# State-space parameters rebuilt: masks in ScalarE's copies, powers multiplied together, taps of four pairs on column groups, chunk matrices laid out by DMAs

## The chip, the cores and the metric

The kernel runs on one core of a Trainium2 chip. The metric is device time in microseconds (us) for one execution of the whole program, lower is better. TensorE multiplies matrices out of SBUF into PSUM; VectorE, ScalarE and GpSimd work on tiles; SyncE here only issues DMAs. In the profile these are PE (with PEld for its weight loads), DVE, ACT, POOL and SP. Each engine takes its instructions in program order and waits on semaphores for the others.

## The reference

Two networks run one after the other on 256 tokens of 1024 features. The first has two layers of differential attention and long convolutions. The second has four stages: an attention mixer, a dense feed-forward layer, an S5 state-space mixer and a mixture of eight experts. The change touches what prepares the S5 mixer. Cut to that:

```
def s5_mixer(h, w_in, lam_re, lam_im, log_dt, b_re, b_im, c_re, c_im, d_skip, w_glu, w_o):
    u = h @ w_in
    ug = u.reshape(B, S, 64 groups, 16)          # 64 states per group
    dt = exp(log_dt); mag = exp(lam_re * dt)
    a_re, a_im = mag * cos(lam_im * dt), mag * sin(lam_im * dt)
    f = (a - 1) / lam                            # complex
    bb = f[..., None] * b                        # complex, per group 64 x 16
    x[t] = a * x[t - 1] + bb @ ug[t]             # complex, by associative scan
    y = real part of (c @ x) + d_skip * u
    y = gelu(y); y = y * sigmoid(y @ w_glu)
    return y @ w_o
```

The kernel does not scan over 256 tokens. It takes four tokens as one step (64 steps), so it needs, for each pair of groups (128 states, 32 channels), matrices made of powers of `a`: input matrices `a^(3-s) * bb` for the tokens s = 0..3 of a step, output matrices `c * a^(t+1)`, and inside a step the taps `c * a^j * bb` for j = 0..3, with `d_skip` added at j = 0.

## The kernel before

All products with weights are done three times (high by high, high by low, low by high part), so each 128x1024 piece of a weight goes through one queue of work: a DMA on SP into `raw`, a copy on ACT into `whi` (L208), a subtraction on DVE into `wlo` (L211), then TensorE.

The dense feed-forward stage (`dense_ffn`) runs over eleven chunks of 256 hidden columns. For each it multiplies for gate and up (`proj_T`, L323 to L325, matmuls of 256 columns) and down (`mm3`, L221 to L223, 512 columns). Its four output accumulators hold four of the five PSUM buffers named `B`, so one is left for everything else. At the end of `proj_T` and of each down chunk a tick gives other generators a turn.

`s5_params` is such a generator. It is started with the stage at 0.7 steps to a tick and builds, for each quarter q of the 32 group pairs (8 pairs), four tables that are stored to DRAM and read back in the S5 stage behind it: sB (input matrices), sC (output matrices), sK (taps laid out as a 128x128 block triangular matrix per pair) and sT (rotations). One quarter before the change:

- `W`: the products of the powers with `bb`, by four calls of `cmul` (six DVE instructions each) on 128x128 elements; `W2` is a copy of `W` on ACT (L1467) for both groups of a pair.
- sB: 16 transposes of `W2` on TensorE (L1472), four to a PSUM buffer, taken out by DVE with a multiplication by a mask (L1474).
- sC: four more `cmul`, and 16 masked copies on ACT (L1488).
- sK: 16 matmuls of `W2` (128 weight columns) with the masked `c` (`s5cmk`, 32 columns) on TensorE (L1500), masked by DVE into `kj`; the skip term added there; a memset of `K` on POOL (L1515), and 10 copies of 32 partitions on ACT and DVE (L1520) that place the taps in the block triangle. One DMA from SP's queue stores it.
- sT: six levels of `cmul`, doubling the length, and a copy on ACT (L1531).

The modulation work of the first network (`adaln`, L959) is of interest too: there, too, a product of 32 weight columns by 128 moving columns is spread over four column groups of the array. Its small results go out by four DMAs from POOL's queue at a time (L965).

The tile framework orders instructions by a simulated time line, so code that is changed in one generator can also move its neighbours. The instructions of each engine keep the order it has chosen.

Of the kernel before, what the change touches and what calls it, by code (L numbers as in the profile page):

```python
# [15 lines left out]
ALU = mybir.AluOpType  # L16
# [102 lines left out]
class Net:  # L119
# [1261 lines left out]
    def s5_steps(self, sp, tp):  # L1381
# [59 lines left out]
        self.s5k = fr, fi, pw, sa, ca, mg4  # L1441

    def s5_params(self, sp):
# [4 lines left out]
        fr, fi, pw, sa, ca, mg4 = self.s5k  # L1448
        bm = self.load(sp, a["s5mask"], [P, 2, P], "s5mask", eng=self.dq)
        eye = self.load(sp, a["eye32"], [32, 32], "eye32", eng=self.dq)  # L1450
        dsk = self.load(sp, a["s5d"], [32, G], "s5d", eng=self.dq)
        for q in range(4):
# [5 lines left out]
            W = self.t(sp, [P, 2, 8, 4, 16], "s5W", bufs=2)  # L1458
# [9 lines left out]
            B = self.t(sp, [P, 8, 2, P], "s5st", bufs=2)  # L1468
# [10 lines left out]
            C = self.t(sp, [P, 8, 2, 4, 2, 16], "s5st", bufs=2)  # L1479
            m2 = bm[:, 1, :].rearrange("p (t g k) -> p t g k", t=4, g=2)[:, 0]  # L1480
            for t in range(4):
                p = pw[:, t + 1]
                cr, ci = self.t(sp, [P, 8, 16], "s5cr"), self.t(sp, [P, 8, 16], "s5ci")
                self.cmul(sp, [P, 8, 16], bc(p[:, 0, :], 16), bc(p[:, 1, :], 16), craw[:, 0], craw[:, 1], cr, ci, "s5cm",
                          neg_i=True)
                for ri, v in enumerate((cr, ci)):
                    for g in range(2):
                        nc.scalar.activation(C[:, :, ri, t, g, :], v, AF.Copy, scale=m2[:, g, 0:1])  # L1488
            self.dq.dma_start(self.sC[q], C.rearrange("p a b c d e -> p (a b c d e)"))
            yield  # L1490

            cm = self.t(sp, [P, 2, 8, 2, 16], "s5cmk")
            for g in range(2):
                nc.scalar.activation(cm[:, 0, :, g, :], craw[:, 0], AF.Copy, scale=m2[:, g, 0:1])
                V.scalar_tensor_tensor(cm[:, 1, :, g, :], craw[:, 1], -1.0,
                                       m2[:, None, g, :].broadcast_to([P, 8, 16]), ALU.mult, ALU.mult)
# [5 lines left out]
            kj = self.t(sp, [P, 8, 2, 16], "s5kj")  # L1502
            m3 = bm[:, 0, :].rearrange("p (g k) -> p g k", g=2)[:, :, :16]
            for g in range(2):
                V.tensor_tensor(kj[:, :, g, :], pt[:, :S].rearrange("p (i g k) -> p i g k", i=8, g=2)[:, :, g, :],
                                m3[:, None, g, :].broadcast_to([P, 8, 16]), ALU.mult)
            kj = kj.rearrange("p i g k -> p i (g k)")
            dd = self.t(sp, [P, 8, 32], "s5dd")[96:128]
            ey, dq = self.t(sp, [P, 32], "s5ey")[96:128], self.t(sp, [P, 8], "s5dq")[96:128]
            V.tensor_copy(ey, eye)  # L1510
            V.tensor_copy(dq, dsk[:, qs])
            V.tensor_tensor(dd, ey[:, None, :].broadcast_to([32, 8, 32]), dq[:, :, None].broadcast_to([32, 8, 32]), ALU.mult)
            V.tensor_tensor(kj[96:128], kj[96:128], dd, ALU.add)
            K = self.t(sp, [P, 8, P], "s5K")
            nc.gpsimd.memset(K, 0.0)  # L1515
# [556 lines left out]
```

## Time and profile before

| | |
|---|---|
| time, median of 3 runs | 1911.8 us (1909.59 to 1914.67) |
| the profiled execution | 1902.7 us, of which its span is 1900.2 us |
| TensorE (PE) busy | 1818.4 us, 96% of the span |
| VectorE (DVE) busy | 1554.9 us, 82% |
| ScalarE (ACT) busy | 1213.4 us, 64% |
| GpSimd (POOL) busy | 164.6 us, 9% |
| dense feed-forward stage | about 736 to 947 us of the span |
| S5 stage | about 947 to 1080 us, the experts behind it to the end |

Times in the views are counted from the span's start. The busy time of a matmul in the profile is its latency, and matmuls overlap; what one costs in a stream is the distance from its start to the next one's start, which the time line shows. "PEclk" is the clock that TensorE was granted as a share of 2.4 GHz.

### The profile page before, as it was taken

The page shows a single profiled execution, that of the slowest core. Times are in us where ns is not written, and L with a number is a line of the kernel's source. Part 1 is how long each engine was busy: PE and PEld are TensorE (multiplying, and loading weights), DVE is VectorE, ACT ScalarE, POOL GpSimd, SP SyncE. Part 2 cuts the span into 40 slices and gives each one's busy share as a digit, 9 for nine tenths or more (in the row PEclk, how much of TensorE's full clock was granted, in tenths as well). Part 3 has the DMA queues.
Part 4 walks back from the last instruction along what each step waited for, and adds up shares of the span by engine and source line. Part 5 has one row for each costly group of instructions (what it writes and reads, how often), then busy time and mean ns, then how long its engine had stood idle before and what let it go on. Part 6 is the DMA issues. An engine that isn't in the chain of part 4 may idle for free.

```text
span 1900.2 us, 31269 instructions
## 1 busy us (share of the span) xinstructions
PE 1818.4 (96%) x11358; PEld 1551.7 (82%) x11358; DVE 1554.9 (82%) x2646; ACT 1213.4 (64%) x1708; POOL 164.6 (9%) x297
## 2 busy tenths in 40 slices
PE   7999998999989998999989899999999999999996
PEld 6887776988878778999889788888888888888784
DVE  6887667687558669998678789999999999998996
ACT  5664355564448535555554677887778787877774
POOL 0003232231330000000000100000001000100000
PEclk9999998999999969999988999999999999999998
DMA  7656785876775504787675779999999999999990
GB/s 247 205 153 209 245 286 197 277 259 196 255 242 159 165 22 156 227 270 241 208 284 196 279 266 376 340 355 344 378 342 349 353 377 354 346 369 361 339 352 24
DMA packets 258539, 503.58 MB, mean 265 GB/s; under 512 B 23346, under 2 KB 101108, under 8 KB 256328
## 3 DMA queue, kind: packets, MB, share of 16 engines
q1 hardware_dynamic: 239384, 448.05, 68.7%
q0 software_dynamic: 18992, 53.45, 7.9%
q8 instruction: 91, 1.49, 0.3%
q14 instruction: 72, 0.59, 0.1%
HBM read 485.47 MB, written 15.75 MB: 264 GB/s over the span
## 4 chain that ended last, share of the span: by engine, by line
PE 78%; issue 10%; DVE 6%; DMA 4%; ACT 2%; POOL 0%; POOLq 0%; ACTq 0%; DVEq 0%
PE A L222 12%; PE A L221 12%; PE A L223 12%; PE B L221 6%; PE B L222 6%; PE B L223 6%; PE A L323 4%; PE A L325 4%; PE A L324 4%; PE B L959 2%; DMA rawm<-in_e_mod_mix_w_dram 2%; DVE wlo L211 1%; PE B L1754 1%; PE B L1101 1%; PE B L440 1%
## 5 line engine op out<-in xcount | busy, mean ns | idle before, releaser
L211 DVE TENSOR_TENSOR wlo<-raw,whi 128x1024 fp32r<-128x1024 f32 x777 | 930.8, 1222 | 183.7 <-ACT whi L208 172.0
L208 ACT ACTIVATE whi<-raw 128x1024 fp32r<-128x1024 f32 x777 | 814.3, 1058 | 344.6 <-PE A L223 137.7
L221 PE MATMUL A<-whi,hTh 128*128 128x512 f32 (+1 forms) x752 | 286.7, 389 | 7.5 <-ACT hTh L208 4.9
L222 PE MATMUL A<-wlo,hTh 128*128 128x512 f32 (+1 forms) x752 | 290.0, 386 | 1.3 <-DVE wlo L211 1.0
L223 PE MATMUL A<-whi,hTl 128*128 128x512 f32 (+1 forms) x752 | 287.5, 384 | 0.9 <-DVE hTl L211 0.9
L323 PE MATMUL A<-hTh,whi 128*128 128x256 f32 x864 | 246.2, 285 | 3.5 <-ACT hTh L208 2.6
L325 PE MATMUL A<-hTh,wlo 128*128 128x256 f32 x864 | 245.2, 284 | 0.0
L324 PE MATMUL A<-hTl,whi 128*128 128x256 f32 x864 | 244.1, 283 | 1.0 <-DVE hTl L211 1.0
L221 PEld LDWEIGHTS A<-whi,hTh 128*128 128x128 f32 x752 | 142.9, 190 | 38.8 <-ACT hTh L208 6.1
L323 PEld LDWEIGHTS A<-hTh,whi 128*128 128x128 f32 x864 | 165.4, 192 | 6.9 <-ACT hTh L208 2.8
L222 PEld LDWEIGHTS A<-wlo,hTh 128*128 128x128 f32 x752 | 143.1, 190 | 33.9 <-DVE wlo L211 4.8
L223 PEld LDWEIGHTS A<-whi,hTl 128*128 128x128 f32 x752 | 142.6, 190 | 31.2 <-DVE hTl L211 2.1
L324 PEld LDWEIGHTS A<-hTl,whi 128*128 128x128 f32 x864 | 165.3, 191 | 3.2 <-DVE hTl L211 1.2
L325 PEld LDWEIGHTS A<-hTh,wlo 128*128 128x128 f32 x864 | 165.1, 191 | 1.7 <-issue 1.2
L222 PE MATMUL A<-wlo,xg 128*128 128x512 f32 (+1 forms) x384 | 143.1, 373 | 0.3 <-DVE wlo L211 0.3
L223 PE MATMUL A<-whi,xg 128*128 128x512 f32 (+1 forms) x384 | 142.7, 372 | 0.0
L221 PE MATMUL A<-whi,xg 128*128 128x512 f32 (+1 forms) x384 | 141.2, 375 | 0.0
L222 PE MATMUL B<-wlo,mhh 128*128 128x512 f32 x352 | 138.6, 394 | 0.0
L223 PE MATMUL B<-whi,mhl 128*128 128x512 f32 x352 | 137.5, 391 | 0.0
L221 PE MATMUL B<-whi,mhh 128*128 128x512 f32 x352 | 120.6, 393 | 0.2 <-ACT mhh L208 0.2
L222 PEld LDWEIGHTS A<-wlo,xg 128*128 128x128 f32 x384 | 72.3, 188 | 13.4 <-DVE wlo L211 0.8
L223 PEld LDWEIGHTS A<-whi,xg 128*128 128x128 f32 x384 | 72.3, 188 | 12.5
(588 smaller groups left out, 2868.9 us busy)
## 6 DMA issues: line engine op xcount, KB each, us to landing
raw<-in_o_exp_up_dram SPq DMA_DIRECT2D x176, 512.0 KB, 5.7
raw<-in_o_exp_down_dram SPq DMA_DIRECT2D x176, 512.0 KB, 6.0
raw<-in_o_exp_gate_dram SPq DMA_DIRECT2D x174, 512.0 KB, 5.8
raw<-in_w_in_dram SPq DMA_DIRECT2D x96, 512.0 KB, 4.8
rawm<-in_e_mod_mix_w_dram POOLq DMA_DIRECT2D x24, 512.0 KB, 6.0
rawm<-in_e_mod_ffn_w_dram POOLq DMA_DIRECT2D x24, 512.0 KB, 5.7
rawm<-in_o_mod_mix_w_dram POOLq DMA_DIRECT2D x24, 512.0 KB, 5.6
rawm<-in_o_mod_ffn_w_dram POOLq DMA_DIRECT2D x24, 512.0 KB, 6.3
```

The costliest lines, as they stand in the source:

```text
L208: nc.scalar.activation(hi, src, AF.Copy)
L211: (nc.gpsimd if lo_eng == "pool" else nc.vector).tensor_tensor(lo, src, hi.bitcast(F32), ALU.subtract)
L221: nc.tensor.matmul(out, ah, bh, start=first, stop=False)
L222: nc.tensor.matmul(out, ah, bl, start=False, stop=False)
L223: nc.tensor.matmul(out, al, bh, start=False, stop=last)
L323: nc.tensor.matmul(o, wh[:, ms], xh[:, k, :], start=k == 0 and m == 0, stop=False, **kw)
L324: nc.tensor.matmul(o, wh[:, ms], xl[:, k, :], start=False, stop=False, **kw)
L325: nc.tensor.matmul(o, wl[:, ms], xh[:, k, :], start=False, stop=k == 7, **kw)
L440: nc.tensor.matmul(o, x[:, ks], dg, start=True, stop=True)
L959: nc.tensor.matmul(acc[32 * j:32 * j + 32, cs], silu[:, k:k + 1].broadcast_to([P, 32]), raws[i][:, k * P:(k + 1) * P], start=r == 0 and i ...
L1101: nc.tensor.matmul(pt[:, i, :], z[ps, ts], w[ps, ts], start=True, stop=True)
L1754: nc.tensor.transpose(ptr[:, i * P:(i + 1) * P], sg[:, i * P:(i + 1) * P], self.ident)
```

## The change

`s5_params` is rewritten, with one more table (`pr`, the powers in falling order) made at the end of `s5_steps`, and with new layouts of three small inputs (mask, unit matrix, skip weights).

- The masks for the two groups of a pair move into ACT's copies of `W` and `C` as a scale per partition (the helper `copy`). DVE's masked eviction of the transposes becomes a plain copy on ACT.
- The three powers of `W`, and the four of `C`, are multiplied in one `cmul` each, on 384 and 512 elements.
- The taps take 32 columns of `W2` as weights and 128 columns of `C` (now with a fifth slot for power 0) as moving data, and four pairs write to the four groups of 32 PSUM partitions.
- The block triangle is no longer built in SBUF. `K` holds three zero blocks and four taps per pair, and 16 DMAs on POOL's queue write shifted windows of it to sK.
- sT is built for two quarters at a time (`TQ = 2`), sC is stored by two DMAs.

```diff
+        pr = self.t(sp, [P, 2, G, 3], "s5pr")
+        for s in range(3):
+            V.tensor_copy(pr[:, :, :, s], pw[:, 3 - s])
...
+        copy = lambda o, i, m: nc.scalar.activation(o, i, AF.Copy, scale=gm[:, m:m + 1])
...
+            shape = [P, 8, 3, 16]
+            p = [pr[:, ri, qs, :, None].broadcast_to(shape) for ri in range(2)]
+            w = [W[:, ri, :, 3:4, :].broadcast_to(shape) for ri in range(2)]
+            self.cmul(sp, shape, *p, *w, W[:, 0, :, 0:3, :], W[:, 1, :, 0:3, :], "s5cw")
             yield
-            for s in range(3):
-                p = pw[:, 3 - s]
-                self.cmul(sp, [P, 8, 16], bc(p[:, 0, :], 16), bc(p[:, 1, :], 16), W[:, 0, :, 3, :], W[:, 1, :, 3, :],
-                          W[:, 0, :, s, :], W[:, 1, :, s, :], "s5cm")
...
             for g in range(2):
-                nc.scalar.copy(W2[:, :, :, :, g, :], W)
+                copy(W2[:, :, :, :, g, :], W, g)
...
-                V.tensor_tensor(B[:, i:i + 2].rearrange("p a b c -> p (a b) c"), pt.rearrange("p (n c) -> p n c", n=4),
-                                bm[:, None, 0, :].broadcast_to([P, 4, P]), ALU.mult)
+                nc.scalar.copy(B[:, i:i + 2].rearrange("p a b c -> p (a b) c"), pt.rearrange("p (n c) -> p n c", n=4))
...
+            self.cmul(sp, shape, *p, *c, cr, ci, "s5cw", neg_i=True)
+            for ri, v in enumerate((cr, ci)):
+                for g in range(2):
+                    copy(C[:, :, ri, 0, g, :], craw[:, ri], 2 * ri + g)
+                    copy(C[:, :, ri, 1:5, g, :], v, g)
+            for ri in range(2):
+                self.dq.dma_start(self.sC[q].rearrange("p (i r m) -> p i r m", i=8, r=2)[:, :, ri],
+                                  C[:, :, ri, 1:5].rearrange("p i t g k -> p i (t g k)"))
...
-            for i in range(8):
-                for ri in range(2):
-                    nc.tensor.matmul(pt[:, i * 32:(i + 1) * 32], W2[:, ri, i].rearrange("p s g k -> p (s g k)"),
-                                     cm[:, ri, i].rearrange("p g k -> p (g k)"), start=ri == 0, stop=ri == 1)
+            for h in range(2):
+                for ri in range(2):
+                    for i in range(4):
+                        nc.tensor.matmul(pt[32 * i:32 * i + 32, h * P:(h + 1) * P], W2[:, ri, 4 * h + i, 3].rearrange("p g k -> p (g k)"),
+                                         C[:, 4 * h + i, ri, 0:4].rearrange("p t g k -> p (t g k)"), start=ri == 0, stop=ri == 1,
+                                         skip_group_check=True)
+            K = self.t(sp, [P, 2, 7, 32], "s5K")
+            nc.gpsimd.memset(K[:, :, 0:3], 0.0)
+            nc.scalar.copy(K[:, :, 3:7], pt[:, :S].rearrange("p (h t m) -> p h t m", h=2, t=4))
+            for h in range(2):
+                V.scalar_tensor_tensor(K[:, h, 3], eye, dsk[:, 2 * q + h:2 * q + h + 1], K[:, h, 3], ALU.mult, ALU.add)
             for s in range(4):
-                for t in range(s, 4):
-                    j = 3 - (t - s)
-                    dst, src = K[s * 32:(s + 1) * 32, :, t * 32:(t + 1) * 32], kj[j * 32:(j + 1) * 32]
-                    (nc.scalar.copy if (s + t) % 2 else V.tensor_copy)(dst, src)
-            self.dq.dma_start(self.sK[q], K.rearrange("p a b -> p (a b)"))
+                for i in range(4):
+                    self.mq.dma_start(self.sK[q][s * 32:(s + 1) * 32].rearrange("k (h i m) -> k i h m", h=2, i=4)[:, i],
+                                      K[i * 32:(i + 1) * 32, :, 3 - s:7 - s].rearrange("k h t m -> k h (t m)"))
```

The order moves in three places of the feed-forward stage. First TensorE, third quarter: before, the taps (`s5cmk` by `s5W2`) stand between a down chunk (`B`, `fhh`) and a gate chunk (`A`, `hTh`).

```order
L221 MATMUL B_1607_8030<-whi_2000_9936,fhh_1987_9863 128x512
L222 MATMUL B_1607_8030<-wlo_2001_9937,fhh_1987_9863 128x512
L223 MATMUL B_1607_8030<-whi_2000_9936,fhl_1988_9864 128x512
L1500 MATMUL B_2003_9969<-s5cmk_2002_9964,s5W2_1948_9704 128x32 x16
L323 MATMUL A_2015_10021<-hTh_1575_7905,whi_2010_10011 128x256
L324 MATMUL A_2015_10021<-hTl_1576_7906,whi_2010_10011 128x256
```

The same place in the changed kernel:

```order
L221 MATMUL B_1608_8034<-whi_1888_9672,fhh_1875_9599 128x512
L222 MATMUL B_1608_8034<-wlo_1889_9673,fhh_1875_9599 128x512
L223 MATMUL B_1608_8034<-whi_1888_9672,fhl_1876_9600 128x512
L1505 MATMUL B_1890_9700<-s5C_1867_9573,s5W2_1854_9483 32x128 x16
L323 MATMUL A_1898_9750<-hTh_1576_7909,whi_1893_9740 128x256
L324 MATMUL A_1898_9750<-hTl_1577_7910,whi_1893_9740 128x256
```

The count (16) and the neighbours are the same; the shape turns from 128x32 to 32x128, and the masked `c` is now the first four slots of `C`.

Next ScalarE, third quarter, before: the weight copies (`whi`) stand among the masked copies that build sC in `s5st`.

```order
L208 ACTIVATE whi_1993_9875<-raw_1992_9873 128x1024
L1488 ACTIVATE s5st_1961_9794<-s5cr_1962_9795,s5mask_1641_8290 128x8x16 x2
L1488 ACTIVATE s5st_1961_9794<-s5ci_1963_9796,s5mask_1641_8290 128x8x16 x2
L1488 ACTIVATE s5st_1961_9794<-s5cr_1968_9811,s5mask_1641_8290 128x8x16 x2
L208 ACTIVATE whi_1997_9930<-raw_1996_9928 128x1024
```

In the changed kernel the copies that stand there, one to a weight copy, empty the PSUM buffers `B` of the transposes:

```order
L1481 COPY s5st_1855_9486<-B_1856_9487 128x512
L208 ACTIVATE whi_1881_9611<-raw_1880_9609 128x1024
L1481 COPY s5st_1855_9486<-B_1857_9493 128x512
L208 ACTIVATE whi_1885_9666<-raw_1884_9664 128x1024
L1481 COPY s5st_1855_9486<-B_1858_9499 128x512
L208 ACTIVATE whi_1888_9672<-raw_1887_9670 128x1024
```

ACT now releases the one free PSUM buffer, which DVE did before. On TensorE the groups of four transposes that take that buffer have 24 to 34 other matmuls between them within a quarter in the changed kernel (the first group of the second quarter is drawn out over more).

Last GpSimd at the end of the stage, before: after the last memset of `K` it goes on with the gate row of the S5 stage (`mgt`) and the first columns of its states (`s5X`).

```order
L1515 MEMSET s5K_2008_9996 128x1024
L1515 MEMSET s5K_2143_10638 128x1024
L201 DMA mgt_2224_10973<-rowo_mod_mix_776_3924 128x1024
L1585 MEMSET s5X0_2257_11179 128x8
L1585 MEMSET s5X1_2258_11180 128x8
```

The same place in the changed kernel:

```order
L1515 DMA sK_1313_6708<-s5K_1891_9717 64x1x128 x16
L1509 MEMSET s5K_2005_10358 128x2x96
L1515 DMA sK_1313_6708<-s5K_2005_10358 64x1x128 x16
L201 DMA mgt_2051_10567<-rowo_mod_mix_776_3924 128x1024
L1587 MEMSET s5X0_2084_10773 128x8
L1587 MEMSET s5X1_2085_10774 128x8
```

Sixteen DMAs per quarter now stand ahead of these on POOL's queue; the last taps on TensorE stand 48 rows, all of them down matmuls of 512 columns, ahead of the end of the stage (before, 95 rows).

## Rows read from the trace of the kernel before

**Rows 1.** The page's first part: busy us, share of the span, number of instructions.

```profile
PE 1818.4 (96%) x11358; PEld 1551.7 (82%) x11358; DVE 1554.9 (82%) x2646; ACT 1213.4 (64%) x1708; POOL 164.6 (9%) x297
```

**Rows 2.** Window: busy us of PE, PEld, DVE, ACT, POOL; clock; DMA; GB/s.

```profile
740.00:940.00 200.00, 200.00 (x1464) 189.38 (x1463) 172.84 (x490) 114.06 (x183) 3.65 (x12) 0.98 0.72 234
```

**Rows 3.** Groups by line in that stage: | busy us, mean ns | idle.

```profile
L323 PE MATMUL A<-hTh,whi 128*128 128x256 f32 x320 | 91.7, 287 | 0.0
...
L211 DVE TENSOR_TENSOR wlo<-raw,whi 128x1024 fp32r<-128x1024 f32 x66 | 80.7, 1222 | 19.3 <-ACT whi L208 18.9
L208 ACT ACTIVATE whi<-raw 128x1024 fp32r<-128x1024 f32 x66 | 69.8, 1059 | 66.9 <-PE A L324 22.6 <-issue 22.2 <-PE B L223 12.1
...
L1500 PE MATMUL B<-s5cmk,s5W 128*128 128x32 f32 x128 | 14.9, 276 | 0.0
L1474 DVE TENSOR_TENSOR s5st<-B,s5mask 128x512 f32<-128x512 f32 x16 | 11.0, 686 | 1.8 <-PE B L1472 1.8
L1488 ACT ACTIVATE s5st<-s5cr,s5mask 128x128 f32<-128x128 f32 x32 | 11.0, 390 | 0.7 <-DVE s5cr L1345 0.7
...
L208 ACT ACTIVATE fhh<-sg 128x512 fp32r<-128x512 f32 x10 | 6.2, 622 | 3.1 <-DVE sg L1296 3.1
```

**Rows 4.** Time line of PE around the third taps: start us, busy us, instruction.

```profile
880.22 0.40 PE L223 MATMUL B<-whi,fhl 128*128 128x512 f32 x1
880.46 3.65 PE L1500 MATMUL B<-s5cmk,s5W 128*128 128x32 f32 x32
883.95 0.36 PE L323 MATMUL A<-hTh,whi 128*128 128x256 f32 x1
884.15 0.28 PE L324 MATMUL A<-hTl,whi 128*128 128x256 f32 x1
```

**Rows 5.** Time line of PE around one burst of the modulation work.

```profile
543.84 0.40 PE L223 MATMUL A<-whi,hTl 128*128 128x512 f32 x1
544.17 1.52 PE L959 MATMUL B<-rawm,silu 128*32 128x128 f32 x48
545.62 0.50 PE L221 MATMUL A<-whi,hTh 128*128 128x512 f32 x1
545.95 0.40 PE L222 MATMUL A<-wlo,hTh 128*128 128x512 f32 x1
```

**Rows 6.** Time line of PE at and behind the first and the last taps.

```profile
785.99 3.89 PE L1500 MATMUL B<-s5cmk,s5W 128*128 128x32 f32 x32
789.70 0.56 PE L323 MATMUL A<-hTh,whi 128*128 128x256 f32 x1
...
792.77 0.28 PE L325 MATMUL A<-hTh,wlo 128*128 128x256 f32 x1
...
929.17 0.37 PE L325 MATMUL A<-hTh,wlo 128*128 128x256 f32 x1
...
932.71 0.28 PE L324 MATMUL A<-hTl,whi 128*128 128x256 f32 x1
```

**Rows 7.** Windows as in rows 2: modulation work, and behind the first taps.

```profile
310.00:560.00 250.00, 248.84 (x2234) 211.46 (x2233) 169.31 (x312) 129.89 (x214) 68.83 (x134) 1.00 0.75 249
...
790.00:795.00 5.00, 5.00 (x34) 5.00 (x34) 4.89 (x19) 3.29 (x7) 0.00 (x0) 0.73 0.56 187
```

**Rows 8.** Durations ns min/median/max: POOL's small DMAs, later readers; the stage's last matmul.

```profile
L965 POOL DMA_DIRECT2D adp<-ads x128: 497/508/520, 142.2 to 559.5; - x128
...
DMA to landing us min/median/max: 2.7/6.0/9.3
...
L195 SPq DMA_DIRECT2D sqK<-sK x4: 320/381/560, 954.2 to 1015.6; - x4
...
L1598 PE MATMUL B<-s5X,sqC x64: 217/275/421, 992.8 to 1043.9; 128*128 128x64 f32 x64
...
946.66 0.40 PE L223 MATMUL B<-whi,fhl 128*128 128x512 f32 x1
```

**Rows 9.** The page's third part: packets, MB, share of 16 engines.

```profile
q1 hardware_dynamic: 239384, 448.05, 68.7%
```

More of the change, by code (lines that the diff above doesn't have):

```diff
@@ L1440, in s5_steps @@
             self.cmul(tp, [P, G], pw[:, j - 1, 0, :], pw[:, j - 1, 1, :], ar, ai, pw[:, j, 0, :], pw[:, j, 1, :], "s5cs")
[L1441 removed]
+        pr = self.t(sp, [P, 2, G, 3], "s5pr")
+        for s in range(3):
+            V.tensor_copy(pr[:, :, :, s], pw[:, 3 - s])
+        self.s5k = fr, fi, pw, pr, sa, ca, mg4
     def s5_params(self, sp):
@@ L1447, in s5_params @@
         G = 32
[L1448 to L1451, printed above, removed]
+        fr, fi, pw, pr, sa, ca, mg4 = self.s5k
+        gm = self.load(sp, a["s5mask"], [P, 4], "s5mask", eng=self.dq)
+        eye = self.load(sp, a["eye32"], [P, 32], "eye32", eng=self.dq)
+        dsk = self.load(sp, a["s5d"], [P, 8], "s5d", eng=self.dq)
+        copy = lambda o, i, m: nc.scalar.activation(o, i, AF.Copy, scale=gm[:, m:m + 1])
         for q in range(4):
@@ L1477, in s5_params @@
             yield
[L1479 to L1488, printed above, removed]
@@ L1489, in s5_params @@
-            self.dq.dma_start(self.sC[q], C.rearrange("p a b c d e -> p (a b c d e)"))
-            yield
[L1492 to L1496, printed above, removed]
+            C = self.t(sp, [P, 8, 2, 5, 2, 16], "s5C")
@@ new lines, in s5_params @@
+            shape = [P, 8, 4, 16]
+            p = [pw[:, 1:5, ri, qs].rearrange("p t i -> p i t")[:, :, :, None].broadcast_to(shape) for ri in range(2)]
+            c = [craw[:, ri, :, None, :].broadcast_to(shape) for ri in range(2)]
+            cr, ci = self.t(sp, shape, "s5cr"), self.t(sp, shape, "s5ci")
+            self.cmul(sp, shape, *p, *c, cr, ci, "s5cw", neg_i=True)
[3 more added lines that the diff above has]
+                    copy(C[:, :, ri, 1:5, g, :], v, g)
@@ L1502, in s5_params @@
[L1502 to L1509, printed above, removed]
@@ L1521, in s5_params @@
-            self.dq.dma_start(self.sK[q], K.rearrange("p a b -> p (a b)"))
-            yield
-            T = self.t(sp, [P, 3, 8, 64], "s5T", bufs=1)
-            nc.gpsimd.memset(T[:, 0, :, 0:1], 1.0)
-            nc.gpsimd.memset(T[:, 1, :, 0:1], 0.0)
-            for k in range(6):
-                n = 1 << k
-                self.cmul(sp, [P, 8, n], T[:, 0, :, :n], T[:, 1, :, :n], bc(ca[:, k + 1, :], n), bc(sa[:, k + 1, :], n),
-                          T[:, 0, :, n:2 * n], T[:, 1, :, n:2 * n], f"s5rt")
@@ new lines, in s5_params @@
+            yield
+            if q % TQ == 0:
+                n8 = 8 * TQ
+                T = self.t(sp, [P, 3, n8, 64], "s5T", bufs=1)
+                nc.gpsimd.memset(T[:, 0, :, 0:1], 1.0)
+                nc.gpsimd.memset(T[:, 1, :, 0:1], 0.0)
+                ts = slice(q * 8, q * 8 + n8)
+                bt = lambda v, n: v[:, ts, None].broadcast_to([P, n8, n])
+                for k in range(6):
+                    n = 1 << k
+                    self.cmul(sp, [P, n8, n], T[:, 0, :, :n], T[:, 1, :, :n], bt(ca[:, k + 1, :], n), bt(sa[:, k + 1, :], n),
+                              T[:, 0, :, n:2 * n], T[:, 1, :, n:2 * n], "s5cw")
+                    if k == 4:
+                        yield
+                nc.scalar.copy(T[:, 2], bt(mg4, 64))
+                nc.gpsimd.memset(T[:, 2, :, 0:1], 0.0)
+                for k in range(TQ):
+                    self.dq.dma_start(self.sT[q + k].rearrange("p (a i c) -> p a i c", a=3, i=8), T[:, :, 8 * k:8 * k + 8])
+                yield
@@ L2008, in layout @@
     tri = np.arange(P)
-    rows, cols = np.arange(P) // 16 % 2, np.arange(P) // 64
-    off = (rows[:, None] == cols[None, :]).astype(np.float32)
+    cols = np.arange(P) // 64
+    off = np.stack([cols == 0, cols == 1], axis=1).astype(np.float32)
     a.update({
@@ L2014, in layout @@
         "s5c": c(np.stack([per_state(g(k).swapaxes(1, 2)) for k in ("o_c_re", "o_c_im")], axis=1)),
-        "s5d": c(g("o_d_skip").reshape(32, 32).T),
-        "s5mask": c(np.stack([off, off.T], axis=1)),
-        "eye32": np.eye(32, dtype=np.float32),
+        "s5d": c(g("o_d_skip").reshape(4, 2, 4, 32).transpose(2, 3, 0, 1).reshape(P, 8)),
+        "s5mask": c(np.concatenate([off, -off], axis=1)),
+        "eye32": np.tile(np.eye(32, dtype=np.float32), (4, 1)),
         "iota": c(np.broadcast_to(np.arange(P + 1, dtype=np.float32), (P, P + 1))),
@@ L2045 @@
     return np.asarray(r.results[0]["out_0_dram"]).reshape(1, S, D)
+TQ = 2
 GATES = 1
```

14 lines of the change are left out of this document (2 added, 12 removed).

## The prediction

> **What bounds the kernel now.** I read the page's totals first, then the one stage in which the changed code runs, then single places of its time line. Over the whole span TensorE is busy for 96% and VectorE for 82% [rows 1], which says nothing yet of the dense feed-forward stage. There the window of 200 us shows TensorE busy for 200.00, VectorE for 172.84, ScalarE for 114.06, DMA at 0.72 [rows 2]. A busy TensorE need not be at its peak, so the time line decides: in this stage plain matmuls of 256 columns start every 0.117 us and those of 512 every 0.233 (880.22 to 880.46 is 0.24), also while VectorE is full, and the groups have 0.0 idle ahead of them [rows 3, 4]. ScalarE's weight copies, on the other hand, wait 66.9 us in sum, mostly for TensorE to hand back their buffers, and VectorE's subtractions wait for ScalarE [rows 3]. So TensorE's own stream sets the end of this stage, and the queue that feeds it has slack. What the change takes off VectorE is therefore worth nothing by itself; what it takes off TensorE's stream is worth its full length, as long as nothing else comes last.
>
> **The change part by part.**
>
> Taps. Before, 16 matmuls of fp32 per quarter, which the profile counts as 32, occupy the stream from 880.46 to 883.95, 3.49 us, and the next matmul takes 0.20 to its neighbour where 0.117 is normal, 0.08 more [rows 4]: 3.57 us, four times, 14.3 us. After, there are again 16 (32 in the profile), with 32 weight columns and 128 moving columns, neighbours on different column groups. The trace has that shape: a burst of the modulation work, 48 matmuls of 128x128 by 32 columns, runs from 544.17 to 545.62, 1.45 us or 30 ns each; the matmul ahead of it and the one behind it take 0.33 to their next where 0.233 is normal, 0.20 together [rows 5]. So 32 cost 0.97 + 0.20 = 1.17 us, four times 4.7. Gain: 14.3 - 4.7 = 9.6 us. Bounds: if the groups did not overlap, each would cost what it does now (0.109 us) and the gain is 0; above, the 0.20 could vanish, which adds 0.8. I take 9.6, since the shape, the order over groups and the type are those of the row.
>
> A rule that speaks against it: the Trainium skill, TensorEngine Tiling (Array Packing), section Key Properties, says that a change of the tiling mode drains TensorE, and there are two such changes around each burst. The row's 0.20 us is what entry and exit cost here, so the trace agrees and the drain is in the sum. The same page's table of theoretical speedup gives up to 4 for 32 columns, an estimate of 0.87 us for a burst without entry and exit.
>
> Clock. Behind the first taps the matmuls are spaced 0.213 us until 792.77: 14 of them from 789.70 take 3.07 us in place of 1.64, and the taps themselves took 3.71 in place of 3.49. Behind the last taps 17 from 929.17 to 932.71 take 3.54 in place of 1.99 [rows 6]. The granted clock there is 0.73 of full speed as the mean of a window with 1.2 GHz first and 2.4 GHz then [rows 7]; what TensorE did before it fell was the long burst of 32-column matmuls. Behind the bursts of the modulation work it does not fall: over 250 us that hold many of them the granted clock is 1.00 [rows 7]. So with the new shape I expect the two spells to go: 1.43 + 0.22 + 1.55 = 3.2 us, of which 0.08 is the exit already counted: 3.1. Bounds: 0 if other spells come, 3.1 if none do. I take 3.1, by the row of the same shape.
>
> VectorE. It loses the 16 masked evictions (11.0 us [rows 3]), the block copies and the fixed cost of many small instructions. This is hidden under TensorE's stream, so 0. If that cover were gone, VectorE would still be the lighter for it; there is no loss to bound.
>
> ScalarE. It gains 16 plain evictions of 512 columns, priced by its copy of that size at 0.62 us: 10 us; the 64 masked copies at 0.39, 25 us, become 16 of 128 columns at 0.39 and 16 of 512 at 0.62, 16 us [rows 3]. In sum it stays near 114 of 200 us. What is new is where it stands: its eviction now frees the only spare PSUM buffer, and TensorE's next group of transposes queues behind that, with the whole feed-forward stream behind it. At least 24 other matmuls stand between two groups, 24 x 0.117 = 2.8 us, while ScalarE needs a weight copy that may be in front (1.06) and the eviction (0.62), 1.7 us. Cost 0, with 1.1 us to spare at each place. If the cover fails: below, among the rivals.
>
> The block triangle by DMAs. SP's queue loses the four DMAs of sK and has eight of sC in place of four: the same number, no price. POOL's queue gets 64. The nearest row is the modulation work's small DMAs from POOL: 0.508 us each at the median, 0.520 at most over 128, and 6.0 us to land, 9.3 at most [rows 8]. Sixteen take 8.1 us and have landed 17 us after the first at worst. The last quarter's taps stand 48 matmuls of 0.233 ahead of the end, 11 us, so its table is in DRAM about 7 us after the stage's last matmul (946.66). The last of the four reads of sK is issued at 1015.6, 69 us after it, and the first reads, at 954.2, concern a table finished long before [rows 8]. Behind the DMAs on POOL stand the gate row and the memsets of the states' first columns, which TensorE uses from 992.8 on, 46 us after the stage [rows 8]. Cost 0.
>
> Here the Trainium skill, SBUF — State Buffer, in its warning on VectorE and DMAs of the GpSimd queue, says that such DMAs wait for descriptors while VectorE runs in a two-port mode: some 3100 ns in place of 620. By that figure sixteen would be an estimate of 50 us, and POOL would come to the memsets 40 us after the stage, just in time; the sum would be the same and the margin nearly gone. The trace speaks against it: none of 128 issues took over 0.520 us, though VectorE was busy for 169 of 250 us in that stretch [rows 7, 8].
>
> DMA volume. The bytes stay, the pieces shrink: sC and sK are now stored in 12,288 pieces of 512 bytes. Lower bound 0. Upper bound: at the mean price of a packet on the hardware queue, 0.687 x 16 x 1900.2 / 239,384 = 0.087 us [rows 9], they take 1,070 engine-us or 67 us of all 16; over 200 us the share would go from 0.72 to 1.05, and the weights would come last by 10 us. I take 0: that mean is of packets of 1.9 KB, and in this stage, with its pieces of 1 KB among others, an engine moves 234 / (16 x 0.72) = 20.3 GB/s [rows 2], hardly less than the mean's 21.5, so a piece costs about by its bytes.
>
> Sum: 9.6 + 3.1 = 12.7 us off the stage. Everything behind is released by its end, and the later stages hold the same work, so it should reach the end of the program. The profiled execution took 1902.7 us, of which 2.5 lie outside the span; it is 0.5% quicker than the median of the runs, 1911.8. I carry the 12.7 us over as they are: 1890.0 for a profiled execution like it, 1911.8 - 12.7 = 1899.1 for the median.
>
> **The rivals.**
>
> 1. The taps get short, but TensorE's clock still falls twice in the stage or falls elsewhere. For it: two of four taps were followed by a spell and two were not, so it hangs on little. Against: the modulation rows. 1911.8 - 9.6 = 1902.2.
>
> 2. No change. Either the column groups do not overlap (against it: 30 ns a matmul in the modulation's rows), or the 12,288 small pieces make the weights late by the 10 us of the upper bound, or the scheduler's small reordering in the expert stage gives the gain back. 1911.8 - 12.7 + 10 to 12.7, about 1910.
>
> 3. Slower: ScalarE comes late to the spare PSUM buffer. Place: the 20 fillings of that buffer (16 groups of transposes, 4 of taps). It decides as soon as ScalarE runs more than the 1.1 us behind which I found to spare. Price: one weight copy of 1.06 us at each plus the eviction, 20 x 1.68 = 34 us if at all of them: 1911.8 - 12.7 + 34 = 1933; at half of them 1916. For it: ScalarE's order is fixed and its copies of `W` and `C` come in blocks (two of 1024 columns, four of 128 and four of 512: by the rows above 2 x 1.06 + 4 x 0.39 + 4 x 0.62 = 6.2 us). Against: it waits for TensorE 66.9 us in the stage now, so it is ahead, not behind.
>
> 4. More than forecast, by stalls that the modelled ends of matmuls hide: 1892.
>
> **How the numbers follow.** Forecast (1899.1): 0.50. Rival 1 (1902.2): 0.17. Rival 4: 0.05. Rival 2: 0.18, of which 0.02 ends beyond the bound below on the faster side. Rival 3: 0.10, a fifth of it so mild that it ends within the bound. The measurement tells about 0.3%, 5.7 us, from no change. Faster by more: 0.50 + 0.17 + 0.05 + 0.02 = 0.74; slower by more: 0.08; within: 0.18. The range reaches from 1893 (the forecast less the 0.8 us of the bound and the 3 us by which runs lie off their median) to 1908 (rival 1 with the same spread and the gentle part of rival 2), which leaves out about 2 in 10.
>
> **What would show it.** In the changed profile the taps (L1505) should take about 1 us per quarter, the clock stay at full in the stage, the stage last about 198 us in place of 211, and no TensorE idle time be put down to ScalarE's eviction (L1481). VectorE's busy time in the stage should fall by far more than the stage gets shorter. The forecast is wrong if the taps' matmuls are spaced over 0.1 us, if TensorE's spacing of 0.117 breaks ahead of transposes, or if the gain is there at the end of the stage and gone at the end of the program.

## The result

The changed kernel takes 1893.5 us at the median (1882.3 to 1896.5, 4 runs) against 1911.9 for the kernel before. The ratio of all runs is 0.9884 with a 95% interval of 0.9842 to 0.9926. A second session gave 1892.2 against 1909.9 us and a ratio of 0.9904 (0.9884 to 0.9924), 18.3 us less (14.5 to 22.2).

So it is faster, as forecast, and by more than forecast: 12.7 us were expected. The predicted 1899.1 us lies 5.6 and 6.9 us above the two measured medians. The first median, 1893.5, is just inside the range that ends at 1893 below; the second, and the first ratio times 1911.9 us (1889.7), are below it.

### The profile page after: what moved, and what is told of

Same layout as the page of the kernel before. It is cut to its first block, busy times and chain, and to the rows that moved or that the text cites. A ratio compares the mean times of both kernels' runs of the same rounds, so it can differ in the third digit from the quotient of the medians.

```text
span 1880.4 us, 31046 instructions
## 1 busy us (share of the span) xinstructions
PE 1803.7 (96%) x11358; PEld 1536.1 (82%) x11358; DVE 1517.6 (81%) x2393; ACT 1210.3 (64%) x1670; POOL 195.9 (10%) x355
## 4 chain that ended last, share of the span: by engine, by line
PE 79%; issue 10%; DVE 5%; DMA 3%; ACT 2%; POOL 1%; POOLq 0%; ACTq 0%; DVEq 0%
PE A L221 12%; PE A L222 12%; PE A L223 12%; PE B L221 6%; PE B L222 6%; PE B L223 6%; PE A L323 4%; PE A L324 4%; PE A L325 4%; PE B L959 2%; DMA rawm<-in_e_mod_mix_w_dram 2%; DVE wlo L211 1%; PE B L440 1%; PE B L1756 1%; PE B L1101 1%
## 5 line engine op out<-in xcount | busy, mean ns | idle before, releaser
L211 DVE TENSOR_TENSOR wlo<-raw,whi 128x1024 fp32r<-128x1024 f32 x777 | 930.3, 1221 | 204.6 <-ACT whi L208 193.1
```

The source lines that it names most:

```text
L211: (nc.gpsimd if lo_eng == "pool" else nc.vector).tensor_tensor(lo, src, hi.bitcast(F32), ALU.subtract)
```

## The profile after

First the page's total of the changed kernel's first profile, beside [rows 1]: TensorE has the same 11,358 matmuls, VectorE 253 instructions fewer, GpSimd 58 more.

```profile
PE 1803.7 (96%) x11358; PEld 1536.1 (82%) x11358; DVE 1517.6 (81%) x2393; ACT 1210.3 (64%) x1670; POOL 195.9 (10%) x355
```

Next the feed-forward stage as one window, from the start of its first gate matmul to the start of its last down matmul, with the columns of [rows 2]: length, busy us of PE, PEld, DVE, ACT and POOL, granted clock, DMA share, GB/s. First the kernel before in a second profile, then the changed kernel.

```profile
755.17:951.87 196.70, 196.70 (x1421) 184.82 (x1420) 169.23 (x455) 113.53 (x185) 3.65 (x12) 0.99 0.72 238
```

```profile
744.32:929.97 185.65, 185.65 (x1421) 172.05 (x1420) 133.32 (x221) 108.17 (x145) 34.48 (x70) 1.00 0.79 252
```

TensorE is busy without a gap in both, and the stage is 11.05 us shorter. VectorE loses 36 us there and is now busy for 133 of 186, without TensorE waiting a moment less than before: it had not waited at all.

The time line of TensorE around the third taps answers to [rows 4].

```profile
869.85 0.40 PE L223 MATMUL B<-whi,fhl 128*128 128x512 f32 x1
870.18 1.08 PE L1505 MATMUL B<-s5C,s5W 128*32 128x128 f32 x32
871.19 0.39 PE L323 MATMUL A<-hTh,whi 128*128 128x256 f32 x1
871.41 0.28 PE L324 MATMUL A<-hTl,whi 128*128 128x256 f32 x1
```

The 32 matmuls last 1.01 us (870.18 to 871.19) in place of 3.49. The matmul ahead of them takes 0.33 to its next in place of 0.233, the one behind them 0.22 in place of 0.117: 0.10 each for entry and exit, as in [rows 5].

The groups of that stage, with the columns of [rows 3]:

```profile
L211 DVE TENSOR_TENSOR wlo<-raw,whi 128x1024 fp32r<-128x1024 f32 x66 | 80.4, 1222 | 43.1 <-ACT whi L208 43.1
L208 ACT ACTIVATE whi<-raw 128x1024 fp32r<-128x1024 f32 x66 | 69.6, 1058 | 67.6 <-PE A L324 26.8 <-issue 20.6 <-PE B L223 16.4
...
L1515 POOL DMA_DIRECT2D sK<-s5K x64 | 33.6, 666 | 99.6 <-DVE s5K L1512 92.7 <-ACT s5W L1457 3.9 <-issue 2.4
...
L1481 ACT COPY s5st<-B 128x512 f32<-128x512 f32 x16 | 9.3, 582 | 8.5 <-PE B L1479 8.4
...
L1505 PE MATMUL B<-s5C,s5W 128*32 128x128 f32 x128 | 4.3, 276 | 0.0
```

ScalarE's weight copies wait 67.6 us, as much as before, and its evictions (L1481) wait for TensorE, not the other way round.

Where the time of the whole program went is read by cutting it at marks that both traces have. Two profiles of each kernel, us (the marks are starts of matmuls in the trace; up to the stage's first gate matmul both kernels have the same 5,304 matmuls in the same order):

| piece | before | changed |
|---|---|---|
| first matmul to the stage's first gate matmul | 740.0, 747.6 | 736.2, 746.0 |
| of that, at half clock | 71.7, 78.5 | 58.0, 78.5 |
| the stage | 198.2, 196.7 | 185.65, 185.62 |
| last down matmul to the program's last matmul | 936.3, 937.2 | 936.9, 937.0 |
| last matmul to the end of the span | 17.27, 17.27 | 13.46, 13.46 |
| outside the span | 2.5, 2.5 | 1.9, 1.8 |

The stage gave what was forecast. The new piece is the end: 3.8 us in the span, 0.6 to 0.7 outside it. The head goes roughly with the time at half clock that a run happens to have: 736.2 us with 58.0 of it, 747.6 with 78.5, but not closely, for at 71.7 us it was anything from 740.0 (before) to 746.3 (tiny32). That is part of why the changed kernel's first profile looks 20 us faster. The runs of one kernel lie as far apart, and also go with the clock: in the second session the kernel before took 1898.6 us at a granted clock of 0.969 and 1917.2 at 0.960.

## The experiments

**The same two kernels again.** Both ran once more without an edit, beside the two kernels that follow.

> The kernel before, unchanged, once more. Between the two profiles that exist the last matmul is 16.3 us earlier after the change, of which 12.3 fall in the dense feed-forward stage and 4.0 ahead of it, where both kernels have the same TensorE order; the end behind the last matmul is 3.8 us shorter. Theory A (the forecast's sum is right and the rest is chance): this profile shows its own clock spells ahead of 315 us, so that its stage begins up to 4 us earlier or later than in the first profile, the stage again lasts 211 us, the end behind the last matmul varies by some us, and the time is 1.000 of before. Theory B (the change saves 5 to 6 us outside the stage in every run): head and end repeat those of the first profile within 1 us.

> The changed kernel once more. Theory A: 0.9935 of before (12.7 us less), stage of 198.5 us, taps 1.0 us per quarter, no clock spell behind the taps. Theory B: 0.9905 of before (18 us less), with the same 198.5 us in the stage and 5 to 6 us less outside it.

Measured: before2 0.9989 of before (0.9967 to 1.0010), after2 0.9904 (0.9884 to 0.9924). The head of before2 is 7.7 us longer than in the first profile, so the head varies without any edit, as theory A said. The end does not: it is 17.27 us twice before and 13.46 twice after. Each theory was right on one of the two places. The first line of SyncE's time line, which has the span, and its last row, the last output DMA; before2 and then after2:

```profile
core 0 of [0], span 1906.3 us
...
1896.71 0.38 SPq L1872 DMA_DIRECT2D out_dram<-hh  x1
```

```profile
core 0 of [0], span 1890.0 us
...
1884.07 0.38 SPq L1874 DMA_DIRECT2D out_dram<-hh  x1
```

From the end of that issue to the end of the span it is 9.2 us before (1906.3 - 1897.1) and 5.55 after.

**The taps alone, and all but the taps.** In taps_only the product is turned round, which gives the changed kernel's shape. The taps then lie in another order and cannot be used; the rearrangement behind them is left out. The edit, cut to its matmuls:

```diff
...
-                    nc.tensor.matmul(pt[:, i * 32:(i + 1) * 32], W2[:, ri, i].rearrange("p s g k -> p (s g k)"),
-                                     cm[:, ri, i].rearrange("p g k -> p (g k)"), start=ri == 0, stop=ri == 1)
...
+                        nc.tensor.matmul(pt[32 * i:32 * i + 32, h * P:(h + 1) * P], cm[:, ri, 4 * h + i].rearrange("p g k -> p (g k)"),
+                                         W2[:, ri, 4 * h + i].rearrange("p s g k -> p (s g k)"), start=ri == 0, stop=ri == 1,
+                                         skip_group_check=True)
```

In taps_old the changed kernel gets `C[:, i, ri, 0:4]` (128 columns) as weights and `W2[:, ri, i, 3]` (32 columns) as moving data; its taps, too, are in another order and not usable.

> The kernel before with the taps alone in the new shape: 32 weight columns, 128 moving columns, four pairs on four column groups. The result lies transposed in PSUM and the masked copies behind it are left as they were, so the taps are not usable: what is left out is that rearrangement. VectorE, ScalarE and the DMAs keep their old work. Theory A: all of the gain in the stage comes with it: stage 198.5 us, taps 1.0 us per quarter, no spells of half clock behind them, 0.9935 of before. Theory B: the same stage, and the 5 to 6 us more of the full change are missing. Rival (the lighter VectorE and ScalarE also count): stage over 202 us.

> The changed kernel with the taps in the old shape (128 weight columns, 32 moving columns); the taps then lie in another order in PSUM and are not usable, the rest of the work is that of the change. Theory A: the gain is gone: stage 208 to 211 us (208 if only the clock spells stay away, 211 if both come back), taps 3.5 us per quarter, 0.998 to 1.000 of before. Theory B: 5 to 6 us stay gained outside the stage: 0.997. Rival (the lighter engines count): stage under 205 us.

Measured: taps_only 0.9939 (0.9923 to 0.9955), taps_old 0.9963 (0.9945 to 0.9980). The stage as a window, taps_only and then taps_old:

```profile
756.80:942.52 185.72, 185.72 (x1422) 172.47 (x1420) 167.62 (x455) 113.18 (x185) 3.65 (x12) 1.00 0.76 253
```

```profile
753.73:950.41 196.68, 196.68 (x1422) 184.87 (x1420) 133.36 (x221) 108.53 (x145) 34.67 (x70) 0.99 0.76 238
```

All of the stage's gain comes with the taps' shape, with VectorE at its old 168 us; with the old shape and a VectorE that does only 133 us the stage is as long as before. The lighter engines are worth nothing there. taps_only ends 17.27 us behind its last matmul, like the kernel before, and taps_old 13.48, like the changed one, so the end belongs to the rest of the change. By their times, taps_only gains 11.6 us (8.6 to 14.7) and taps_old 7.1 (3.8 to 10.5), an interval that holds the 4.5 us that its end and the time outside the span give.

**Is the end a matter of where code lies?** SyncE's records show a pause of 1.64 us between two semaphore waits in the end of before2, which after2 lacks, and the instruction queue has one more 8 KB packet right behind it. SyncE's DMAs are 901 in both kernels, but the changed one has eight semaphore waits more. pad_sp adds eight DMAs of 128 bytes on SyncE, pad_both ten memsets on GpSimd as well:

```diff
+        pad = self.t(sp, [P, 512], "s5pad", bufs=1)
+        for k in range(8):
+            self.dq.dma_start(pad[0:1, 32 * k:32 * k + 32], a["eye32"][0:1, 0:32])
+        for k in range(10):
+            nc.gpsimd.memset(pad[:, 448 + k:449 + k], 0.0)
```

> The first runs put the part of the gain that was not forecast at the very end: behind the last issue of an output DMA the span lasts 9.2 us in the kernel before and in taps_only, and 5.5 us in the changed kernel and in taps_old. There SyncE stands still for 1.65 us between two semaphore waits and GpSimd for 2 us in its last drain, each beside one more 8 KB packet on the instruction queue. Theory C (code placement): the end of each engine's code is fetched in blocks, and the change moves the block's border out of the final stretch by adding 8 instructions to SyncE's stream and 66 to GpSimd's. This kernel is the kernel before with eight DMAs of 128 bytes more on SyncE's queue in the feed-forward stage (SyncE's stream grows by 8, GpSimd's by 1). Expected by C: SyncE's 1.65 us are gone, so 7.5 us behind the last output DMA (5.5 if the one instruction more moves GpSimd's border too), ratio 0.998 to 0.999. Theory D (the end is shorter because of what the change computes or stores): 9.2 us stay, ratio 1.000.

> As pad_sp, with ten tiny memsets on GpSimd more (its stream grows by 11). Expected by C: both stalls gone, 5.5 us behind the last output DMA, as in the changed kernel, 4 to 4.5 us less time in all: ratio 0.9977. By D: 9.2 us, ratio 1.000. The stage stays as in the kernel before, about 197 to 198 us from its first gate matmul to its last down matmul.

Measured: 0.9993 (0.9978 to 1.0009) and 1.0000 (0.9984 to 1.0017). SyncE's pause is gone in both (no gap above 0.08 us between its semaphore waits), and still 9.2 us lie behind the last output DMA. Theory C fits the pause and fails for the end. Over all the traces of this document the pause (1.1 to 1.7 us) is there where SyncE has 1732 to 1741 instructions and gone from 1748 on; that a border in the code lies at that place is a reading of the extra packet and was not tested by itself. The records of the end then show who comes last: GpSimd, whose last long drain (an instruction named DRAIN at the end of the engine's stream) lasts 9.78 us in every kernel so far without the 64 DMAs on its queue and 5.13 with them.

**ScalarE's eviction and GpSimd's DMAs.** evict_dve gives the 16 evictions back to VectorE, k_on_sp moves the 64 DMAs of the block triangle to SyncE's queue:

```diff
-                nc.scalar.copy(B[:, i:i + 2].rearrange("p a b c -> p (a b) c"), pt.rearrange("p (n c) -> p n c", n=4))
+                V.tensor_copy(B[:, i:i + 2].rearrange("p a b c -> p (a b) c"), pt.rearrange("p (n c) -> p n c", n=4))
```

```diff
-                    self.mq.dma_start(self.sK[q][s * 32:(s + 1) * 32].rearrange("k (h i m) -> k i h m", h=2, i=4)[:, i],
+                    self.dq.dma_start(self.sK[q][s * 32:(s + 1) * 32].rearrange("k (h i m) -> k i h m", h=2, i=4)[:, i],
```

> The changed kernel with the 16 evictions of the transposes back on VectorE, as plain copies. The forecast priced ScalarE's eviction at zero, with 1.1 us to spare at each place. If that is right: the stage lasts 185.6 us from its first gate matmul to its last down matmul, as in the changed kernel, within 0.5 us, and the time is 0.990 of before, as the changed kernel's. If ScalarE does come late at some of the 20 places, up to 1.7 us each, this kernel is the faster one: stage under 185, ratio under 0.989.

> The changed kernel with the 64 DMAs that lay out the block triangle on SyncE's queue in place of GpSimd's. Sixteen of them, at 0.34 to 0.42 us an issue, stand for about 6 us per quarter ahead of weight loads. If the queue of weights has the slack that the forecast gave it: stage 185.6 us within 1 us and 0.990 to 0.991 of before. Rival (the weights come late behind each quarter): TensorE waits for whi or wlo, stage 188 to 195 us, ratio 0.992 to 0.995. By theory C the end behind the last output DMA stays near 5.5 us on SyncE's side (its stream is 57 longer than the changed kernel's), and GpSimd's 2 us may come back (its stream is only 2 longer than before).

Measured: evict_dve 0.9909 (0.9886 to 0.9933) with a stage of 185.67 us: the price of zero for ScalarE's eviction holds. k_on_sp 0.9957 (0.9940 to 0.9975) with a stage of 192.46 us, in which TensorE is idle for 5.13. The two stages as windows:

```profile
755.71:941.38 185.67, 185.67 (x1421) 172.08 (x1420) 142.54 (x237) 99.80 (x129) 34.42 (x70) 1.00 0.78 252
```

```profile
751.98:944.44 192.46, 187.33 (x1422) 173.38 (x1420) 133.36 (x221) 107.90 (x145) 1.08 (x6) 0.99 0.76 242
```

The rows of k_on_sp show a rival of the prediction at work. SyncE's time line, then ScalarE's, then TensorE's, each in one stretch between the second quarter's taps and the third's (start, us, what; in brackets the idle time ahead and what ended it):

```profile
844.62 0.40 SPq L265 DMA_DIRECT2D raw<-in_e_ffn_up_dram  x1
845.12 13.86 SPq L1515 DMA_DIRECT2D sK<-s5K  x16
859.08 1.27 SPq L1496 DMA_DIRECT2D sC<-s5C  x2
860.44 1.23 SPq L265 DMA_DIRECT2D raw<-in_e_ffn_up_dram  x1
```

```profile
856.79 1.06 ACT L208 ACTIVATE whi<-raw 128x1024 fp32r<-128x1024 f32 x1 [1.37 <-issue]
867.10 1.06 ACT L208 ACTIVATE whi<-raw 128x1024 fp32r<-128x1024 f32 x1 [9.26 <-DMA raw<-in_e_ffn_up_dram]
868.06 0.57 ACT L1481 COPY s5st<-B 128x512 f32<-128x512 f32 x1
```

```profile
868.68 1.12 PE L1479 MATMUL B<-ident,s5W 128*128 128x128 f32 x4 [5.13 <-ACT s5st L1481]
```

The 16 DMAs hold SyncE's queue for 13.86 us (not the 6 that I had expected), the next weight is asked for 15 us late, ScalarE stands 9.26 us in front of it with the eviction queued behind, and TensorE waits 5.13 us for that eviction, because it frees the only spare PSUM buffer. A spell of 3.4 us at half clock (1.2 GHz) follows; together the stage is 6.8 us longer. In the changed kernel no weight copy waits for a DMA in the stage, and nothing of this happens. The end of k_on_sp is again long (9.5 us behind the last output DMA), with GpSimd's drain at 9.78.

**What sets GpSimd's last drain.** pool64 and pool4 store the old `K` of the kernel before from GpSimd's queue, in 16 DMAs per quarter or in one; pool_tiny adds 64 DMAs of one piece of 128 bytes; taps_pool64 is taps_only and pool64 together. The edits of pool64 and, without the line that makes `pad`, of pool_tiny:

```diff
-            self.dq.dma_start(self.sK[q], K.rearrange("p a b -> p (a b)"))
+            for s in range(4):
+                for i in range(4):
+                    self.mq.dma_start(self.sK[q][s * 32:(s + 1) * 32, i * 256:(i + 1) * 256],
+                                      K[s * 32:(s + 1) * 32, 2 * i:2 * i + 2].rearrange("p a b -> p (a b)"))
```

```diff
...
+            for k in range(16):
+                self.mq.dma_start(pad[q * 32:q * 32 + 1, 32 * k:32 * k + 32], a["eye32"][0:1, 0:32])
```

> The padded kernels refuted theory C for the larger part: SyncE's stall of 1.65 us went away, but the end stayed, because GpSimd's last drain lasts 9.8 us (until 8.8 us behind the last output DMA) in every kernel without the 64 DMAs on GpSimd's queue, also in k_on_sp, and 5.1 us (until 3.0) in the three kernels with them. Theory E: that drain depends on what GpSimd's software DMA queue has carried in the run. This kernel is the kernel before with its sK stored by 16 DMAs per quarter (32 pieces of 1 KB each) on GpSimd's queue in place of one on SyncE's. By E: drain of about 5 us in place of 9.8, 5.5 to 7.2 us behind the last output DMA (7.2 if SyncE's own 1.65 us stay), ratio 0.998; the stage as in the kernel before, 197 to 198 us. Theory F (it is something else of the changed kernel, as its lighter VectorE or its layouts in DRAM): 9.8 and 9.2 us stay, ratio 1.000.

> As pool64, with one DMA per quarter (128 pieces of 2 KB) on GpSimd's queue: four DMAs more in place of 64. If E holds through the number of DMAs, 4 more change nothing (drain 9.8 us, 1.000); if through the pieces or bytes, the drain is shorter by part or all of the 4.7 us.

> The kernel before with 64 DMAs of one piece of 128 bytes more on GpSimd's queue, 16 per quarter, all other work as it was. If E holds through the number of DMAs: drain about 5 us, 7.2 us or less behind the last output DMA, ratio 0.998. If through the pieces: drain 9.8, ratio 1.000.

> taps_only and pool64 together (its taps lie in another order and are not usable, as in taps_only). If the gain of the change is the taps in the stage (11 to 12.6 us) plus the drain (3.7 us, less what SyncE's 1.65 us keep): 14 to 17 us, ratio 0.991 to 0.9925, equal to the changed kernel's 0.9904 within the intervals, with all of the old work on VectorE. If E is wrong: 0.994 as taps_only.

Measured: pool64 0.9990 (0.9971 to 1.0009), pool4 1.0001 (0.9986 to 1.0017), pool_tiny 0.9994 (0.9978 to 1.0010), taps_pool64 0.9927 (0.9906 to 0.9947). The two us at the end are too little for the times to tell, so the records of the end decide, and they do not vary: 5.13 us of drain with 64 DMAs more, of 32 pieces or of one, and 10.11 with four more, where I had expected no change. VectorE's load and the layouts in DRAM have no part in it (theory F falls). taps_pool64 has the stage of 185.76 us and ends 14.84 us behind its last matmul in place of 17.27, still with SyncE's pause. It lies 15.3 us below before by the medians and 13.9 by the ratio, so its time lies between those of taps_only and the whole change and is not apart from either; that taps and drain together give most of the gain rests on the records.

pool_tiny with 16, 32, 96 and 128 DMAs in place of 64 tells whether more DMAs are better. Each of the four ran once, so only their records are read.

> As pool_tiny, with 16 one-piece DMAs more on GpSimd's queue in place of 64 (256 in all, by 32 packets each 19,504 packets). So far GpSimd's last drain took 9.78 us at 18,992 packets on its queue, 10.11 at 19,568 and 5.13 at 21,040. Theory E1 (the drain grows with what the queue carried since some border, and starts low again behind it): 10.0 to 10.1 us. Theory E2 (it falls step by step with more DMAs): 8 to 9 us.

> As pool_tiny with 32 DMAs more (272 in all, 20,016 packets). E1: 10.3 to 10.4 us, or already about 4.5 us if the border lies in between. E2: 7 to 8 us.

> As pool_tiny with 96 DMAs more (336 in all, 22,064 packets). E1: 5.7 us, longer than the 5.13 us at 64, by 0.33 us for each 576 packets. E2: under 5.13 us.

> As pool_tiny with 128 DMAs more (368 in all, 23,088 packets). E1: 6.3 us. E2: under 5 us, the less the more DMAs.

The records of the end, us (drain: length of GpSimd's last long drain; its end, the end of SyncE's own drain ahead of the engines' last exchange of semaphores, and the span's end are counted from the end of the last output DMA's issue):

```
kernel      GpSimd's DMAs   drain   drain's end   SyncE's drain        span's end
before2         240          9.78      8.41             6.40              9.24
pad_sp          240          9.78      8.41             4.75              9.24
k_on_sp         240          9.78      8.41             4.73              9.54
pool4           244         10.11      8.83             5.94              9.95
tiny16          256          1.21     -2.26             6.38              7.21
tiny32          272          2.51     -0.63             6.40              7.23
pool_tiny       304          5.13      2.62             6.47              7.29
pool64          304          5.13      2.63             6.24              7.05
after2          304          5.13      2.64             4.74              5.56
tiny96          336          7.74      5.87             6.29              7.10
tiny128         368         10.35      9.13             6.35             10.41
```

The drain grows by 0.082 us with each DMA ((10.35 - 1.21) / 112) and starts low again somewhere between 244 and 256. So E1 is right in kind and E2 falls. E1's numbers I had wrong (10.0 to 10.1 us for tiny16, which has 1.21; 6.3 for tiny128, which has 10.35): the drain goes by DMAs, not by packets. Four DMAs of 576 packets in all add 0.33 us (pool4), sixteen of 512 packets in all 1.31 (tiny16 to tiny32). The instruction ahead of the drain, INC_SWDGE_SEM, grows too, from 0.45 us in tiny16 to 2.68 in tiny128, and is 2.54 in before2 and 1.41 in after2; so the drain's end moves by 0.10 us with each DMA. The span ends 0.8 to 1.3 us behind the later of GpSimd's drain and SyncE's. The changed kernel is short on both: 64 more DMAs put the drain at 5.13, and eight more instructions on SyncE take away the 1.64 us pause. The drain alone gives about 2 us (9.24 to 7.05 and 7.29), the pause the rest (to 5.56). Both are luck of a count: tiny128, with 64 DMAs more than that, has the worst end of all. The first and the last line of SyncE's time line in tiny16 and in tiny128:

```profile
core 0 of [0], span 1907.0 us
...
1899.42 0.38 SPq L1875 DMA_DIRECT2D out_dram<-hh  x1
```

```profile
core 0 of [0], span 1914.0 us
...
1903.18 0.38 SPq L1875 DMA_DIRECT2D out_dram<-hh  x1
```

## Why the prediction was right in the stage and short at the end

- **What bounds the stage:** right. TensorE's stream sets its end, and VectorE's 36 us are worth nothing (taps_old).
- **Taps:** right. 1.01 us and 0.20 for entry and exit per quarter, 1.21 against 1.17 forecast. With the old shape a stage with 3.4 us at half clock, one spell, takes 196.7 us, with two spells 198.2, with three 199.8 (pool_tiny), with four 201.4 (tiny128), so a spell costs 1.55 us and a stage without any would take 195.15. Against 185.65 that makes 9.5 us for the four taps; 9.6 was forecast.
- **Clock:** right in kind, the size a matter of the run. Every kernel with the new shape and no stall has 1.00 in the stage; those with the old shape have one to four spells, 1.5 to 6.2 us, and each of these spells begins within about 1 us of the end of a burst of old taps. The forecast's 3.1 was the value for the two that its profile happened to have; before2 has one, worth 1.5.
- **VectorE, ScalarE, DMA volume at zero:** right (evict_dve; taps_old, which has the lighter engines and the small pieces and a stage as long as before2's; and a DMA share that rose from 0.72 to 0.79 with no idle TensorE).
- **ScalarE late at the spare PSUM buffer (rival 3):** did not happen in the changed kernel, and is a real mechanism: k_on_sp has it at one place, for 5.13 us in place of the 1.7 that I priced, since what holds ScalarE is a late weight and not one more copy.
- **The block triangle by DMAs:** here the forecast failed. It asked what GpSimd's 64 DMAs delay, found nothing late, and wrote zero, without a bound below. An issue took more than forecast, 0.644 us at the median and 0.947 at most against 0.508 and 0.520 [rows 8], which cost nothing. What it did not ask is what the queue itself does at the program's end. SyncE's queue it called "the same number, no price" by its DMAs; its eight more semaphore waits took the pause away. The same holds for its last step, "I carry the 12.7 us over as they are", with 2.5 us outside the span as if that were fixed. The end gave 3.8 us in the span (GpSimd's drain 9.78 to 5.13, SyncE's pause gone) and 0.65 outside it.

The rows of those issues in the changed kernel (min, median and max ns, first and last start):

```profile
L1515 POOL DMA_DIRECT2D sK<-s5K x64: 511/644/947, 785.1 to 929.2; - x64
...
DMA to landing us min/median/max: 1.9/3.7/6.6
```

The Trainium skill's figure of 3100 ns for a DMA of GpSimd's queue beside a VectorE copy (SBUF — State Buffer, A bandwidth-pool intuition that's wrong) is not seen in these 64 issues, with VectorE busy for 133 of 186 us. The Trainium skill speaks there of a tensor copy, though, and 80.4 of those us are subtractions (L211), so these rows do not test it, and the prediction's rows, which do not say what VectorE ran, speak against it less than it claimed.

So the step that failed is the end of the program, priced at nothing: 4.45 us of gain that the forecast did not have. That they came out as a gain is luck; nothing in the change aims at them. The sum now: 9.5 for the taps, 1.5 to 3.1 for the clock, 3.8 at the end and 0.65 outside make 15.5 to 17.0 us, inside the interval of the second session (14.5 to 22.2). The 1.3 to 2.8 us up to its middle are not found in any piece; the head, which varies from 736 to 751 us over the profiles of all kernels with the same work in it, hides them. Whether they exist stays open.

## What to carry to other kernels

Where TensorE's stream is full, only what shortens that stream counts: find the shape of the new instruction elsewhere in the same trace, take its spacing with entry and exit, and add it up; here the sum for the taps came out to a tenth of a us. Then look at the end of the program too: every engine's last drain and every pause behind the last output, because a change that adds DMAs or instructions to a queue moves it without being near it. And a queue's slack holds for the load that it was read at: the 64 DMAs that cost nothing on GpSimd cost 6.8 us on SyncE, through three engines.

## What the runs showed of the hardware

- GpSimd's last long drain costs 0.082 us for each DMA that its queue has carried, 10.35 us at most here, and starts low again (1.21 us) past some count between 244 and 256. Size and pieces of the DMAs play no part (64 of 128 bytes and 64 of 32 KB: 5.13 us both). What in the queue is counted, and where exactly it starts again, was not tried.
- At the end, behind a taken branch, ScalarE's first instruction came 3.2 us after the branch began, and SyncE paused for a further 1.64 us; eight more instructions ahead on SyncE removed that pause. The Trainium skill (Runtime: NRT & Kernel Launch, Instruction fetch mechanics) says that a taken branch to code that is not yet loaded forces a fetch, and that crossing a border in the code is mostly hidden. The 3.2 us fit the first; if the pause is such a border, which the runs suggest and do not show, it is not hidden right behind a branch.
- The time outside the span is 1.8 to 1.9 us wherever no instruction packet is fetched behind its end (after2, pad_both), 1.8 to 2.3 with one (taps_pool64, pad_sp), 2.1 to 2.5 with two (pool4, before2). So it goes with these packets loosely; what sets it stays open.
- A spell of 3.4 us at half clock costs 1.55 us in a stage where TensorE is full; the bursts with 32 weight columns on four column groups were not followed by one in the stage in any of the four kernels that have them without a stall (granted clock 1.00).
